# Fewer directly computed tiles ahead of the Strassen products in the FFNs of a two-layer trunk

## The chip, the cores and the metric

The kernel runs on one core of a Trainium2 chip, as one program. The metric is device time in microseconds (us). Numbers are float32 in and out.

## The reference

Two layers, each with three residual sub-layers: a SwiGLU feed-forward (FFN 1), a token mixer, and another SwiGLU (FFN 2). There are 512 tokens of width 1024; the inner width of an FFN is 2816.

```
def rms_norm(x, gain):
    inv = lax.rsqrt(jnp.mean(xf * xf, axis=-1, keepdims=True) + EPS)
    return (xf * inv).astype(x.dtype) * gain

def swiglu(h, w_in, w_out):
    gate, up = jnp.split(h @ w_in, 2, axis=-1)
    return (jax.nn.silu(gate) * up) @ w_out

for l in range(DEPTH):
    x = x + 0.5 * swiglu(rms_norm(x, ffn1_norm[l]), ffn1_w_in[l], ffn1_w_out[l])
    h = rms_norm(x, mix_norm[l]) @ w_mix_in[l]
    ...
    x = x + y @ w_mix_out[l]
    x = x + 0.5 * swiglu(rms_norm(x, ffn2_norm[l]), ffn2_w_in[l], ffn2_w_out[l])
```

## The kernel before

**Layout and precision.** The residual stream stands transposed in SBUF as `xT`: eight blocks of 128 channels by 512 tokens. A float32 product is made from two parts of each operand, a rounded high part (a cast on ScalarE, ACT) and the remainder (a subtraction on VectorE, DVE): high by high, high by low and low by high, three matmuls on TensorE (PE). So every weight tile that PE reads first passes ACT and then DVE; the pair lands in one of three buffers called `hl`.

**Two ways through the first matrix of an FFN.** The inner width is 22 tiles of 128, each with a gate and an up half. A pair of tiles can be computed directly, which the kernel calls *covered* (`cover`): 96 matmuls of 512 columns on the un-normalised `x` times the gain, in four steps of 24; the factor 1/rms per token is applied afterwards, when the bank is emptied ("clear", two multiplications by `inv` on DVE, then silu on ACT and "values", two products on DVE). Or a pair is computed as seven products after Strassen and Winograd (`halved`): P1 to P7, each 24 matmuls of 256 columns, 168 in all. These need the normalised `x` in four quarters `xn` (`normalise`), three sums of quarters ("+"), and from these seven operands `xc` (`operand`: a cast on ACT, a remainder on DVE). They also need sums of the weights' quarters q0 to q3: S1 to S4, S2 to S4 on DVE (`total`), and others by DMAs that add from memory (`add`, issued by GpSimd (POOL)).

**The entry of an FFN.** The inverse norm is not known when an FFN starts: the squares of the last channels are still to be summed. The covered tiles go first, because they need only `x`. Meanwhile the sum of squares is taken by a matmul with a matrix of 1/1024 (`squares`, `sum_norm`), then logarithm, exponential and a Newton step make `inv` (`take_norm`, `rsqrt`), and the quarters, sums and operands are made. What is due at which step is written out in the table `ENTRY`, under the number of covered tiles: a step number and a list of jobs. `deal(n)` issues the jobs of step n. While tiles are covered it is called with 2f + k // 2 (tile f, channel block k), four steps a pair; then with 2 * covered + n ahead of the first three weight preparations (`LEAD` = 3), and with the next numbers after each product. "load" starts the first unit of `halved`: four weight quarters by SP's queue, q2, q0, q3, q1 in order, and the addition of q3 to q2 (S1) by POOL's queue; "sum" is S2 on DVE. `prepare` casts one product's weights on ACT and takes its remainder on DVE, three products ahead of PE.

**Counts.** FFN 1 of layer 0 (the *opening*, in which `x` is also loaded and turned) covers six tiles, the three others four. In the opening, the sum of squares comes after the first covered pair; in FFN 1 of layer 1 `mean` = 2 and in FFN 2 `mean` = 3 say at which step it is dealt out.

**Order.** Tile schedules freely what is not tied; the kernel ties much of it: `follow(e, i)` appends instruction i to a hand-written chain of engine e ("a" ACT, "v" DVE, "p" PE, "s" SP's queue, "g" POOL's queue), so that the order of issue on each engine at an entry is that of the code. An instruction that waits therefore holds all that is behind it on its engine. The products of all later units run in an order that a planner (`plan`) made, with loads ahead.

**The opening's start.** Before data arrive PE multiplies zeros (`none`) by zeros (`idle`), two times and once more. The tile `none`, like `inv`, has the tag "inv" in a pool with one buffer per tag. In `norm_part` the square of a channel block is made by ACT into a tile `sq` of the rotating pool with several buffers, and added to `sqacc` by DVE.

Lines of the profile: L378 and L379 are cast and remainder of streamed weights, L392, L398 and L399 the three matmuls, L445 the first rows of the opening, L532 the addition of a square, L551 the sum by matmul, L300 activations (logarithm and exponential among them), L543 the last step of the Newton iteration, L643 and L644 "clear", L752 `normalise`, L774 and L775 ACT's and DVE's part of a negated operand, L816 the transfers that add weights from memory, L829 the sums of weights, L841 and L843 cast and remainder of a product's weights, L859 the addition of S2 to q1 by a transfer, L940 the copy of g2 in a silu.

Of the kernel before, what the change touches and what calls it, by code (L numbers as in the profile page):

```python
# [8 lines left out]
F32 = mybir.dt.float32  # L9
F32R = mybir.dt.float32r  # L10
# [3 lines left out]
AF = mybir.ActivationFunctionType  # L14
ALU = mybir.AluOpType
# [10 lines left out]
P = 128  # L26
T = 512
D = 1024
# [5 lines left out]
CHUNKS = ((0, 8), (8, 8), (16, 6))  # L34


ORDER_IN = ("P1", "P2", "P6", "P5", "P7", "P3", "P4")
ORDER_OUT = ("P2", "P1", "P5", "P6", "P7", "P3", "P4")
LEAD = 3

# [2 lines left out]


ENTRY = {
# [5 lines left out]
    },  # L51
# [5 lines left out]
    },  # L57
}

# [124 lines left out]
class Trunk:  # L184
# [8 lines left out]
    def __init__(self, ctx, tc):  # L193
        self.tc = tc
        self.nc = tc.nc
        nc = self.nc
        self.const = ctx.enter_context(tc.tile_pool(name="const", bufs=1))
        self.res = ctx.enter_context(tc.tile_pool(name="res", bufs=1))
        self.wp = ctx.enter_context(tc.tile_pool(name="wp", bufs=1))
        self.ps = ctx.enter_context(  # L200
            tc.tile_pool(name="ps", bufs=1, space=bass.MemoryType.PSUM)
        )
        self.dram = ctx.enter_context(
            tc.tile_pool(name="dram", bufs=1, space=bass.MemoryType.DRAM)
        )
        self.ident = self.const.tile([P, P], F32, tag="ident", name="ident")
        make_identity(nc, self.ident)
        self.ones_mean = self.const.tile([P, P], F32, tag="ones_mean", name="ones_mean")
        nc.vector.memset(self.ones_mean, 1.0 / D)
        self.epsc = self.const.tile([P, 1], F32, tag="epsc", name="epsc")  # L210
        nc.vector.memset(self.epsc, EPS)
        self.xT = self.res.tile([P, KD, T], F32, tag="xT", name="xT")

        self.none = self.res.tile([P, T], F32R, tag="inv", name="none")
        nc.vector.memset(self.none.bitcast(F32), 0.0)

        self.xh, self.xl = [None] * KD, [None] * KD
        self.uid = 0
        self.ntog = 0
        self.tab, self.tab_users = None, []  # L220
        self.chain = {}

    def build_consts(self, scratch):

# [182 lines left out]
    def stream_steps(  # L407
        self, jobs, parts_of, act, nk, mid=None, pre=None, deal=None, keep=False, lead=False,
        last=False, fine=False, deep=2, rowwise=False,
    ):  # L410

        k = 0
        while k < nk:
            kk = min(deep, nk - k)
            if callable(mid) and k == nk - 2:
                mid()
            st = None
            if pre is not None:  # L430

                if k == 0:
                    st = self.open_rows(parts_of(k, kk), kk)
                pre(k)
            if deal is not None:
                deal(k)
            skew = SKEW_MOVING if jobs[0][2] is not None and jobs[0][0].shape[-1] < T else 0
            if st is not None:

                def first(hi, lo):  # L440

                    ah, al = act(0)
                    for n, (w, x) in enumerate(((hi, ah), (lo, ah), (hi, al))):
                        for acc, cols, _ in jobs:
                            self.follow("p", self.nc.tensor.matmul(  # L445
                                acc, w[:, cols], x, start=n == 0, stop=False, skip_group_check=True
                            ))
                        if n == 0:
                            pre(k, None)

                self.between = first
            rows = self.granule(parts_of(k, kk), kk, pre is None, skew, deal is not None, st)
            if st is not None:
                self.first_rows = self.chain["v"]
            end = k + kk == nk
            halves = end and last
            order = (
                [(job, j) for job in jobs for j in range(kk)]
                if end and not rowwise or lead and k == 0
                else [(job, j) for j in range(kk) for job in jobs]  # L460
            )
            for n, ((acc, cols, toks, *more), j) in enumerate(order):
                if pre is not None and n == len(order) // 2:
                    pre(k, True)
                if fine and n == len(order) // 2:
                    yield
                if pre is not None and k + j == 0:
                    continue
                ah, al = act(k + j)
                hi, lo = rows[j]  # L470
                first, stop = k + j == 0 and not more, end and j == kk - 1
                if toks is None:
                    self.mm3(acc, hi[:, cols], lo[:, cols], ah, al, first, stop, False, keep)
                elif not (halves and acc is jobs[-1][0]):
                    self.mm3(
                        acc, ah[:, toks], al[:, toks], hi[:, cols], lo[:, cols], first, stop, False, keep
                    )
            if halves:
                acc, cols, toks = jobs[-1]
                for c in (slice(0, T // 2), slice(T // 2, T)):  # L480
                    for j in range(kk):
                        ah, al = act(k + j)
                        hi, lo = rows[j]
                        self.mm3(
                            acc[:, c], ah[:, toks], al[:, toks], hi[:, c], lo[:, c], False, j == kk - 1
                        )
            k += kk
            yield
# [20 lines left out]
    def norm_part(self, j, pool, xj=None, part=None):  # L509
# [16 lines left out]
        if j == 0:  # L526
            self.sqacc = self.res.tile([P, T], F32, tag="sqa", name=self.n("sqa"))
            nc.scalar.activation(self.sqacc, xj, AF.Square)
        else:
            sq = pool.tile([P, T], F32, tag=self.tt, name=self.n("sq"), bufs=self.tb)  # L530
            nc.scalar.activation(sq, xj, AF.Square)
            nc.vector.tensor_add(self.sqacc, self.sqacc, sq)  # L532

# [93 lines left out]
    def cover(self, fp, w_in, w_out, covered, mean, begin):  # L627
# [35 lines left out]
        def deal(n):  # L663
            if n == mean and begin is None:
                squares()
            for what in filter(None, ENTRY[covered].get(n, "").split(", ")):
                name, *at = what.split()
                at = [int(v) if v.isdigit() else v for v in at]
                if name == "norm":
# [23 lines left out]
        for f in range(0, covered, 2):  # L693
            banks = self.next4()

            def parts(k, kk, f=f):
# [6 lines left out]
                [(bk, slice(c, c + P), None) for bk, c in zip(banks, (0, 256, 128, 384))],  # L703
                parts, self.xact, KD, None,
                (lambda *a: self.open_x(x, gain, fp, *a)) if opening else None,
                None if opening else (lambda k, f=f: deal(2 * f + k // 2)), begin is None or f > 2,

                lead=f == 2 and begin is not None,
            )
# [71 lines left out]
    def halved(self, fp, w_in, w_out, covered, deal):  # L781
# [49 lines left out]
        def prepare(kind, w, p):  # L831
# [7 lines left out]
            hl = self.wp.tile([P, 2 * 1024 + 64], F32R, tag="hl", name=self.n("hl"), bufs=3)  # L839
            hi, lo = (hl[:, a + SKEW_HELD : a + SKEW_HELD + 1024] for a in (0, 1024))  # L840
            A(nc.scalar.copy(hi, src))  # L841
            parts[u, p] = [a.rearrange("p (k c) -> p k c", k=4) for a in (hi, lo)]
            return lambda: V(nc.vector.tensor_sub(lo, src, hi))  # L843

        def moving(c, p):

# [40 lines left out]
                do[name](*args)  # L887

        u = seq[0][:2]
        for q in (2, 0, 3, 1):  # L890
            raw[u, q] = t = fp.tile(
                [P, 4, 2 * P], F32, tag=("mh", "ml")[q % 2], name=self.n("w"), bufs=2
            )
# [821 lines left out]
    def open_x(self, x, gain, fp, k, loaded=False):  # L1715
# [5 lines left out]
            return  # L1721
        if not loaded:
            if k == 0:
                self.idle(2)
                self.begin_norm(gain, fp)
                self.table(LNEXP)
                self.follow("a", self.tab_ins)
                self.xb = {0: self.load_x(x, 0, fp)}
                self.load_open(0)
                self.idle(1)  # L1730
                self.xb[1] = self.load_x(x, 1, fp, True)
                self.load_open(1)
            self.norm_part(k, fp, self.xb[k], 0)
# [8 lines left out]

    def idle(self, n):

        for _ in range(n):
            b = self.bank("po")
            self.follow("p", self.nc.tensor.matmul(b, self.none[:, :P], self.none, start=True, stop=True))

    def open_rest(self, j, fp):
# [25 lines left out]
def trunk_kernel(  # L1775
# [4 lines left out]
    k = Trunk(ctx, tc)  # L1780
    for l in range(DEPTH):
        k.ffn(
            ffn1_w_in[l], ffn1_w_out[l], mix_norm[l], 4 if l else 6, 2,
            begin=(x, ffn1_norm[0]) if l == 0 else None,
        )
        k.mix(
# [1 line left out]
            fox_k_gain[l], fox_f_bias[l], ffn2_norm[l], hgrn_lb_logits,  # L1788
        )
        k.ffn(  # L1790
            ffn2_w_in[l], ffn2_w_out[l], ffn1_norm[l + 1] if l + 1 < DEPTH else None, 4, 3,
            out=out if l + 1 == DEPTH else None,
        )

# [28 lines left out]
```

## Time and profile before

| what | us |
|---|---|
| median of 3 runs | 1830.18 |
| lowest and highest | 1828.83, 1830.91 |
| the profiled execution, its time | 1832.37 |
| the profiled execution, its span | 1830.6 |

The profile is one execution, taken by the hardware profiler. The span runs from its first to its last instruction. PE is TensorE's matmuls, PEld its weight loads (they run beside matmuls), DVE VectorE, ACT ScalarE, POOL GpSimd, SP SyncE; "x" and a number are instructions. A row of the timeline has the start in us, the duration in us (of all of them, where x4 at the end of the row stands for four in a run), the engine, the line, the operation, the tiles written and read, their sizes, and in brackets how long the engine stood idle before it and what ended that. A row of windows has the stretch, its length, and for each engine asked for (PE alone, or PE, PEld, DVE, ACT and POOL) the busy time and in brackets the number of instructions, then the granted clock of TensorE (1.00 is full), the DMA engines' busy share and the GB/s moved. The mean granted clock was 1.00. The transfers of the whole execution:

```profile
q1 hardware_dynamic: 193904, 192.15, 35.7%
q0 software_dynamic: 55840, 68.19, 23.4%
HBM read 226.15 MB, written 2.17 MB: 125 GB/s over the span
```

q1 are the transfers that SP issues, q0 those that POOL issues: packets, MB, and their share of 16 DMA engines' span.

### The profile page before, as it was taken

How to read it: one execution, taken by the hardware profiler on the slowest of the kernel's cores; microseconds unless marked ns; L12 is line 12 of the kernel's file. 1: busy time of each engine (PE TensorE's matmuls, PEld its weight loads, DVE VectorE, ACT ScalarE, POOL GpSimd, SP SyncE). 2: the span in 40 equal slices, each digit the busy share in tenths (PEclk: the TensorE clock that was granted, in tenths of full speed). 3: DMA queues.
4: the chain of work that ended last, by engine and by line, in shares of the span. 5: the costliest groups of instructions: out<-in, count | busy, mean ns of one | idle time of the engine just before them, and what ended most of it. 6: DMA issues, size and time to landing. Idle time of an engine off the chain costs nothing.

```text
span 1830.6 us, 31999 instructions
## 1 busy us (share of the span) xinstructions
PE 1821.0 (99%) x12934; PEld 1674.7 (91%) x12934; DVE 1445.3 (79%) x1965; ACT 1001.7 (55%) x1414; POOL 185.1 (10%) x190
## 2 busy tenths in 40 slices
PE   9999999999999999999999999999999999999999
PEld 7899999888888899999889999998888888999997
DVE  8889786679677888879678887976777778888883
ACT  5455554465666465555445555555656655555552
POOL 0011120100000101112001111201000001020210
PEclk9999999999999999999999999999999999999999
DMA  7668783242543767868276787823425438677762
GB/s 214 177 134 189 177 180 94 68 124 68 127 110 96 216 136 168 193 165 174 81 202 140 174 183 190 163 69 84 114 74 127 119 98 217 161 152 196 154 135 92
DMA packets 249908, 262.38 MB, mean 143 GB/s; under 512 B 19816, under 2 KB 228464, under 8 KB 249760
## 3 DMA queue, kind: packets, MB, share of 16 engines
q1 hardware_dynamic: 193904, 192.15, 35.7%
q0 software_dynamic: 55840, 68.19, 23.4%
q8 instruction: 101, 1.65, 0.4%
q14 instruction: 47, 0.39, 0.1%
q10 hardware_dynamic: 16, 0.00, 0.0%
HBM read 226.15 MB, written 2.17 MB: 125 GB/s over the span
## 4 chain that ended last, share of the span: by engine, by line
PE 96%; ACT 1%; DVE 1%; DMA 1%; issue 0%; SPq 0%; DVEq 0%; ACTq 0%
PE mm L392 14%; PE mm L399 14%; PE mm L398 14%; PE sc L392 6%; PE sc L399 6%; PE sc L398 6%; PE pt L392 6%; PE pt L399 6%; PE pt L398 6%; PE po L392 4%; PE po L399 4%; PE po L398 4%; PE sc L1600 1%; PE po L1655 1%; PE sc L1414 1%; PE pt L1637 1%
## 5 line engine op out<-in xcount | busy, mean ns | idle before, releaser
L841 ACT CAST hl<-w 128x1024 fp32r<-128x1024 f32 x322 | 337.7, 1050 | 347.6 <-PE mm L399 81.9
L843 DVE TENSOR_TENSOR hl<-w,hl 128x1024 fp32r<-128x1024 f32 x322 | 392.5, 1220 | 87.2 <-ACT hl L841 87.0
L379 DVE TENSOR_TENSOR hl<-st,hl 128x1024 fp32r<-128x1024 f32 (+3 forms) x152 | 160.0, 1053 | 120.4 <-ACT hl L378 119.7
L378 ACT CAST hl<-st 128x1024 fp32r<-128x1024 f32 (+3 forms) x152 | 138.6, 912 | 176.3 <-PE po L399 81.5
L392 PE MATMUL mm<-xc,hl 128*128 128x256 f32 (+1 forms) x730 | 201.4, 276 | 0.3 <-ACT g L940 0.3
L399 PE MATMUL mm<-xc,hl 128*128 128x256 f32 x728 | 201.4, 277 | 0.0
L398 PE MATMUL mm<-xc,hl 128*128 128x256 f32 x728 | 201.2, 276 | 0.0
L392 PE MATMUL sc<-xc,hl 128*128 128x256 f32 (+1 forms) x530 | 146.4, 277 | 0.6 <-ACT g L940 0.6
L399 PE MATMUL sc<-xc,hl 128*128 128x256 f32 x528 | 146.1, 277 | 0.0
L398 PE MATMUL sc<-xc,hl 128*128 128x256 f32 x528 | 146.0, 277 | 0.0
L392 PEld LDWEIGHTS mm<-xc,hl 128*128 128x128 f32 x730 | 137.0, 188 | 0.8 <-ACT g L940 0.5
L398 PEld LDWEIGHTS mm<-xc,hl 128*128 128x128 f32 x728 | 136.8, 188 | 0.0
L399 PEld LDWEIGHTS mm<-xc,hl 128*128 128x128 f32 x728 | 136.6, 188 | 0.1
L392 PE MATMUL pt<-xc,hl 128*128 128x256 f32 (+1 forms) x482 | 132.7, 276 | 0.0
L398 PE MATMUL pt<-xc,hl 128*128 128x256 f32 x480 | 132.7, 276 | 0.0
L399 PE MATMUL pt<-xc,hl 128*128 128x256 f32 x480 | 132.6, 276 | 0.0
L392 PE MATMUL mm<-x,hl 128*128 128x512 f32 x272 | 108.8, 400 | 0.0
L399 PE MATMUL mm<-x,hl 128*128 128x512 f32 x272 | 106.1, 390 | 0.0
L398 PE MATMUL mm<-x,hl 128*128 128x512 f32 x272 | 105.9, 389 | 0.0
L392 PEld LDWEIGHTS sc<-xc,hl 128*128 128x128 f32 x530 | 99.5, 188 | 1.5 <-ACT g L940 1.0
L399 PEld LDWEIGHTS sc<-xc,hl 128*128 128x128 f32 x528 | 99.2, 188 | 0.1
L398 PEld LDWEIGHTS sc<-xc,hl 128*128 128x128 f32 x528 | 99.1, 188 | 0.0
(487 smaller groups left out, 5470.6 us busy)
## 6 DMA issues: line engine op xcount, KB each, us to landing
w<-in_ffn_w_in_dram SPq DMA_DIRECT2D x140, 512.0 KB
w<-in_ffn_w_out_dram SPq DMA_DIRECT2D x64, 512.0 KB
w<-in_ffn_w_out_dram POOLq DMA_DIRECT2D x56, 512.0 KB, 9.0
st<-in_w_mix_in_dram SPq DMA_DIRECT2D x80, 256.0 KB
w<-in_ffn_w_in_dram POOLq DMA_DIRECT2D x39, 512.0 KB, 8.1
st<-in_ffn_w_in_dram SPq DMA_DIRECT2D x70, 256.0 KB
w<-S POOLq DMA_DIRECT2D x35, 512.0 KB, 4.7
st<-in_ffn_w_out_dram SPq DMA_DIRECT2D x24, 512.0 KB
```

The source lines that it names most:

```text
L378: a = nc.scalar.copy(hi, src[:, c : c + w])
L379: b = nc.vector.tensor_sub(lo, src[:, c : c + w], hi)
L392: i = nc.tensor.matmul(acc[:, c], ah, bh[:, c], start=first and c.start == 0, stop=False, skip_group_check=True,)
L398: nc.tensor.matmul(acc, ah, bl, start=False, stop=False, skip_group_check=True)
L399: i = nc.tensor.matmul(acc, al, bh, start=False, stop=last, skip_group_check=True)
L841: A(nc.scalar.copy(hi, src))
L843: return lambda: V(nc.vector.tensor_sub(lo, src, hi))
L1414: nc.tensor.matmul(s2[:, :, t], e[:, i * P : (i + 1) * P], e2[:, :, t], start=True, stop=True)
L1600: mm = lambda *a, **k: E(nc.tensor.matmul(*a, skip_group_check=True, **k))
L1637: E(nc.tensor.transpose(tb[:, k * P : (k + 1) * P], to[u][:, j * P : (j + 1) * P], self.ident))
L1655: E(nc.tensor.matmul(self.ob[:, o], half[2][:, j, h].rearrange("p a d -> p (a d)"), part[:, at[0] : at[-1] + 1, :].rearrange("p b t -> p ( ...
```

## The change

- The opening covers four tiles, not six; the other three FFNs cover two, not four. What is no longer covered goes through the seven products, one pair more in each FFN.
- `ENTRY` has a table for two covered tiles and one named "opening"; the old two are gone. `deal` is also called in the middle of a step (n + 0.5), so that a job can stand at a half step ("load" at 3.5; the sum of squares of layer 1's FFN 1 at `mean` = 1.5). In FFN 2 the sum of squares stands at step 2.
- P5 comes before P6 in the order of products in the first matrix.
- Where two tiles are covered, the remainders of the first two weight preparations (P1 and P2 of the first unit) aren't made by DVE: ACT writes the negated rounded weights to the low part, and a DMA issued by POOL adds the weights to it.
- The first unit's quarters are loaded in the order q2, q0, q1, q3.
- The squares in `norm_part` go to one buffer, that of the tag "inv".
- In the opening the zeros are written first, there are four and three matmuls on them, not two and one, and each group writes one bank, not a new one each time. The chains begin with the zeros' and the ones' memset on DVE.

```diff
-ORDER_IN = ("P1", "P2", "P6", "P5", "P7", "P3", "P4")
+ORDER_IN = ("P1", "P2", "P5", "P6", "P7", "P3", "P4")
...
 ENTRY = {
-    4: {
-        5: "norm, x 0 0", 6: "x 1 0, P1", 7: "load, x 0 1, + 0 0 0 1, P2", 8: "sum, x 1 1, P5",
-        9: "clear 0, + 0 0 1 1", 10: "silu 0, + 0 1 1 1, P6, P7", 11: "values 0, clear 1",
-        12: "silu 1, P3", 13: "+ 0 0 1 0, values 1", 14: "P4", 17: "clear 2", 18: "silu 2",
+    2: {
+        3.5: "load", 4: "norm, x 0 0", 5: "P1, x 1 0", 6: "P2, x 0 1, + 0 0 0 1, P5, sum",
+        7: "x 1 1, + 0 0 1 1, + 0 1 1 1, P6", 8: "P7", 9: "P3, + 0 0 1 0", 10: "P4", 12: "clear 0",
+        13: "silu 0", 14: "values 0, clear 1", 15: "silu 1", 16: "values 1",
+    },
+    "opening": {
+        6: "norm", 7: "load, x 0 0, x 1 0, P1", 8: "x 0 1, + 0 0 0 1, P2", 9: "clear 0, sum",
+        10: "P5, x 1 1", 11: "+ 0 0 1 1, P6, clear 1", 12: "silu 0, + 0 1 1 1, P7", 13: "values 0, P3",
+        14: "silu 1, + 0 0 1 0, P4", 15: "values 1", 17: "clear 2", 18: "silu 2",
         19: "values 2", 20: "clear 3", 21: "silu 3", 22: "values 3",
-    },
-    6: {
-        7: "norm, x 0 0", 8: "x 1 0, clear 0, clear 1", 9: "silu 0, silu 1, x 0 1, P1, + 0 0 0 1",
-        10: "load, P2, values 0, values 1, x 1 1", 11: "P5, clear 2, + 0 0 1 1",
-        12: "silu 2, P6, clear 3, sum", 13: "values 2, silu 3, + 0 1 1 1, P3", 14: "P7, values 3, + 0 0 1 0",
-        15: "P4", 16: "clear 4", 17: "silu 4", 18: "values 4, clear 5", 19: "silu 5", 20: "values 5",
     },
 }
...
+        self.none = self.res.tile([P, T], F32R, tag="inv", name="none")
+        self.follow("v", nc.vector.memset(self.none.bitcast(F32), 0.0))
         self.ident = self.const.tile([P, P], F32, tag="ident", name="ident")
...
-        nc.vector.memset(self.ones_mean, 1.0 / D)
+        self.follow("v", nc.vector.memset(self.ones_mean, 1.0 / D))
...
+                if deal is not None and n == len(order) // 2:
+                    deal(k, 0.5)
...
-            sq = pool.tile([P, T], F32, tag=self.tt, name=self.n("sq"), bufs=self.tb)
+            sq = self.res.tile([P, T], F32, tag="inv", name=self.n("sq"))
             nc.scalar.activation(sq, xj, AF.Square)
             nc.vector.tensor_add(self.sqacc, self.sqacc, sq)
...
             A(nc.scalar.copy(hi, src))
+            byload = covered == 2 and u == seq[0][:2] and p in ("P1", "P2")
+            if byload:
+                A(nc.scalar.activation(lo, src, AF.Copy, scale=-1.0))
+                G(nc.gpsimd.dma_start(lo.bitcast(F32), src, accum_op=ALU.add))
...
-            return lambda: V(nc.vector.tensor_sub(lo, src, hi))
+            return lambda: byload or V(nc.vector.tensor_sub(lo, src, hi))
...
-        for q in (2, 0, 3, 1):
+        for q in (2, 0, 1, 3):
...
-                self.idle(2)
+                self.idle(4)
...
-                self.idle(1)
+                self.idle(3)
...
+        b = self.bank("po")
         for _ in range(n):
-            b = self.bank("po")
...
-            ffn1_w_in[l], ffn1_w_out[l], mix_norm[l], 4 if l else 6, 2,
+            ffn1_w_in[l], ffn1_w_out[l], mix_norm[l], 2 if l else 4, 1.5,
...
-            ffn2_w_in[l], ffn2_w_out[l], ffn1_norm[l + 1] if l + 1 < DEPTH else None, 4, 3,
+            ffn2_w_in[l], ffn2_w_out[l], ffn1_norm[l + 1] if l + 1 < DEPTH else None, 2, 2,
```

More of the change, by code (lines that the diff above doesn't have):

```diff
@@ L196, in __init__ @@
         nc = self.nc
+        self.uid = 0
+        self.ntog = 0
+        self.tab, self.tab_users = None, []
+        self.chain = {}
         self.const = ctx.enter_context(tc.tile_pool(name="const", bufs=1))
@@ L212, in __init__ @@
         self.xT = self.res.tile([P, KD, T], F32, tag="xT", name="xT")
-        self.none = self.res.tile([P, T], F32R, tag="inv", name="none")
-        nc.vector.memset(self.none.bitcast(F32), 0.0)
         self.xh, self.xl = [None] * KD, [None] * KD
[L218 to L221, printed above, removed]
     def build_consts(self, scratch):
@@ L665, in deal @@
                 squares()
-            for what in filter(None, ENTRY[covered].get(n, "").split(", ")):
+            for what in filter(None, ENTRY[covered if begin is None else "opening"].get(n, "").split(", ")):
                 name, *at = what.split()
@@ L705, in cover @@
                 (lambda *a: self.open_x(x, gain, fp, *a)) if opening else None,
-                None if opening else (lambda k, f=f: deal(2 * f + k // 2)), begin is None or f > 2,
+                None if opening else (lambda k, half=0, f=f: deal(2 * f + k // 2 + half)), begin is None or f > 2,
                 lead=f == 2 and begin is not None,
```

## The prediction

> **What bounds the kernel now.** I read the page first (engines, slices, chain), then windows of single stages, then the timeline of one entry into an FFN.
>
> ```profile
> span 1830.6 us, 31999 instructions
> PE 1821.0 (99%) x12934; PEld 1674.7 (91%) x12934; DVE 1445.3 (79%) x1965; ACT 1001.7 (55%) x1414; POOL 185.1 (10%) x190
> PEclk9999999999999999999999999999999999999999
> PE 96%; ACT 1%; DVE 1%; DMA 1%; issue 0%; SPq 0%; DVEq 0%; ACTq 0%
> ```
>
> TensorE (PE) works in 99% of the span and is 96% of the chain of waits: nothing but its matmuls sets the end. So there are two ways to change the time: fewer PE microseconds, or new pauses of PE. The change does the first on purpose; the question is what it does to the second, and for that a 79% share of VectorE (DVE) says little. It has to be read at the entry of an FFN.
>
> ```profile
> 57.14:78.90 21.76, 21.76 (x98) 1.00 0.79 221
> 78.90:98.07 19.17, 19.17 (x170) 1.00 0.48 108
> 593.35:616.00 22.65, 22.65 (x100) 1.00 0.68 194
> 614.78:637.75 22.97, 22.97 (x103) 19.00 (x102) 22.90 (x32) 10.06 (x11) 3.45 (x3) 1.00 0.84 234
> ```
>
> In these windows the first time after the stretch is PE's busy time; in the last row PEld's and then DVE's (22.90) follow. The first row is a pair of covered tiles (96 matmuls of 512 columns), the second a pair in seven products (168 of 256 columns), the third a covered pair with the norm's sum in it. The fourth is the stretch between the finished inverse norm and the first product of layer 0's FFN 2: DVE has 0.07 us free in 23 us. What it does there (normalising, operands, remainders) is what the products need, and two covered pairs give it the time.
>
> **What is saved.** A pair that goes from covered to products saves 21.76 - 19.17 = 2.59 us of PE. Four pairs move (one in each FFN): 10.4 us. The built order agrees: 672 more matmuls of 256 columns (4 x 168) and 384 fewer of 512, beside 4 more on zeros.
>
> **What the shorter cover exposes, FFN 2 of either layer.** Rows of layer 0's entry, PE, ACT and DVE:
>
> ```profile
> 593.35 0.39 PE L392 MATMUL sc<-x,hl 128*128 128x512 f32 x1
> 603.35 0.69 DVE L532 TENSOR_TENSOR sqa<-sqa,sq 128x512 f32<-128x512 f32 x1
> 609.67 1.02 PE L551 MATMUL po<-sqa,ones_mean 128*128 128x512 f32 x2
> 610.79 0.69 ACT L300 ACTIVATE nr<-po,epsc 128x512 f32<-128x512 f32 x1 [5.30 <-PE po L551]
> 613.76 1.28 ACT L293 ACT_TABLE_LOAD   x1
> 614.09 0.69 DVE L543 TENSOR_TENSOR inv<-nr,nt 128x512 f32<-128x512 f32 x1
> 614.81 1.67 DVE L752 SCALAR_TENSOR_TENSOR xn<-xT,gain,inv 128x256 f32<-128x256 f32 x4
> 616.40 1.22 DVE L379 TENSOR_TENSOR hl<-st,hl 128x1024 fp32r<-128x1024 f32 x1
> 616.52 1.06 ACT L774 ACTIVATE xc<-xn 128x1024 fp32r<-128x1024 f32 x1 [1.47 <-DVE xn L752]
> 617.54 1.67 DVE L752 SCALAR_TENSOR_TENSOR xn<-xT,ngain,inv 128x256 f32<-128x256 f32 x4
> 619.12 1.22 DVE L775 SCALAR_TENSOR_TENSOR xc<-xn,xc 128x1024 fp32r<-128x1024 f32 x1
> ```
>
> From starts: four normalising steps take 1.59 (614.81 to 616.40), an operation on 128x1024 takes 1.14 (616.40 to 617.54) and is done after 1.22; ACT's part of an operand is done after 1.06; the logarithm starts 1.12 after the sum (609.67 to 610.79) and the inverse is ready 3.99 after that (614.78).
>
> Count from the start of the cover (593.35 = 0). The sum is now called at step 2 of 4, not 3 of 8: at 10.9, where the last square has just been added (604.04, or 10.7; the squares now share one buffer, so each waits for the addition before it, but only the last one or two by some 0.1). Logarithm 12.0, inverse 16.0. The cover ends at 22.65 (third row of the windows) and the products start there, 2.74 each.
>
> DVE's order is fixed by hand; the built one gives, from the inverse on: normalise (0,0); remainder of operand P1; normalise (1,0); remainder P2; normalise (0,1); an addition; remainder P5; S2; weight remainders P5, P6; normalise (1,1); two additions; remainder P6. That is 4 x 1.59 + 9 x 1.14 + 1.22 = 17.8, and three times DVE stands 1.1 for ACT's half of an operand that has just been normalised: 21.4, with the small gaps 21.7. So P6's operand is whole at 16.0 + 21.7 = 37.7, and P6, the fourth product, wants it at 22.65 + 3 x 2.74 + 0.1 = 31.0: **6.7 late** (P5 takes the first 3 of them). Then P7: its weights are q0 plus a transfer that can only be issued after S2 (30.2).
>
> ```profile
> w<-in_ffn_w_in_dram POOLq DMA_DIRECT2D x39, 512.0 KB, 8.1
> w<-S POOLq DMA_DIRECT2D x35, 512.0 KB, 4.7
> DMA to landing us min/median/max: 4.5/4.7/7.2
> ```
>
> Landed 38.4, cast 39.5, remainder 40.7, and the remainder of operand P7 behind it on DVE 42.3; P7 could start at 40.4: 1.8 more. P4 loses 0.6 in the same way. Sum **9.1 us of new pauses against 2.59 saved: +6.5 for each FFN 2**.
>
> The two remainders made by transfers cost ACT two casts with a sign (1.06 each, by the L774 row) and POOL two issues; the table load that used to lie behind a cast now ends at 15.3, so P1's second cast ends at 17.3. For their landing no row shows a copy of w into hl; the nearest is w<-S, 4.7 in the median (third row: 4.5 to 7.2), and the slowest POOL row, 15.0 for additions from memory, is the far end. At 4.7 P1 and P2 land at 22.1 and 25.4, on time; at 7.2 they are 2 late, and the chain to P6 swallows that. I take 0.
>
> **FFN 1 of layer 1.**
>
> ```profile
> 919.31 0.39 PE L392 MATMUL mm<-x,hl 128*128 128x512 f32 x1
> 925.45 0.68 DVE L532 TENSOR_TENSOR sqa<-sqa,sq 128x512 f32<-128x512 f32 x1
> DMA to landing us min/median/max: 5.7/8.3/15.0
> ```
>
> Here the squares are added at 926.13, 6.8 after the cover's start, and the sum goes out at step 1.5, at 8.2. All of the chain is 2.7 earlier, the transfer of P7 included; where it waited for buffers it gains less: **6.6 of pauses, +4.0 net**.
>
> **The opening (layer 0, FFN 1).**
>
> ```profile
> 34.21 1.04 ACT L378 CAST hl<-st 128x1024 fp32r<-128x1024 f32 x1 [2.18 <-DMA st<-in_ffn_w_in_dram]
> 36.53 0.68 ACT L300 ACTIVATE nr<-po,epsc 128x512 f32<-128x512 f32 x1
> 45.42 0.68 DVE L644 TENSOR_TENSOR ui<-sc,inv 128x512 f32<-128x512 f32 x1
> L445 PE MATMUL sc<-x,hl 128*128 128x512 f32 x6 | 3.5, 680 | 1.0 <-ACT hl L378 1.0
> L398 PE MATMUL sc<-x,hl 128*128 128x512 f32 x14 | 5.5, 390 | 0.0
> ```
>
> The logarithm is moved one cast forward, to 35.3, behind the cast that waits for a load (34.21). The inverse is ready at 39.2. P1 starts at 57.14, after the second covered pair. In the built order DVE has, before P5 may start, the two remainders of the cover, the operands up to P6, weight remainders, S2 and, last, "clear 1", which empties the bank that P5 writes: 13 x 1.14 + 4 x 1.59 + 3 x 0.6 = 23 and 4 of waits for ACT, to 66.3. P5 wants it at 62.6: 3.7 late. P7's addition and operand and P4's come behind: 2.3 more. **6.0 of pauses, +3.4 net.**
>
> The zeros: matmuls of 512 columns took 680 ns before 12.3 us, 390 after. Twelve of them stand there, 0.2 apart in pace, so 2.4 us are to be had at most, and 0 if the clock opens no earlier. But the logarithm hangs on a load (the 2.18 of the L378 row), so a faster PE meets the same 66.3 unless loads come earlier too. I take half, -1.2, and keep 0 and -2.9 (with the transposes) as ends. Loads, the additions' order and the buffer of the squares elsewhere I cost at nothing: PE hides them, and where DVE has no slack they are in the chains above. In the pairs behind an entry DVE catches up (some 17 of 19 us); 0, up to 0.5 an entry.
>
> **Sum.** 2 x 9.1 + 6.6 + 6.0 - 10.4 - 1.2 = **+19.2 us**. The profiled execution has a span of 1830.6 and a time of 1832.37; the median of the runs is 1830.18, 0.4 below that span. I put the change on the median: **1849.4**.
>
> **Rivals.**
>
> *The lead suffices (faster).* If the operands were ready when PE asks, only the saving stays: 1830.18 - 10.4 - 1.2 = 1818.6. For it: the sum is as early as the squares allow, two DVE operations are gone from the entry, and PE has no long wait today. Against: it needs 30 us less lateness over four entries, and the order of DVE with durations seen in dozens of rows leaves little room; it decides at 2.9 of pauses an entry. 14%.
>
> *Half and half.* P6's lateness stays, the rest is hidden, and the zeros pay: 2 x 6.7 + 4 + 3.7 - 10.4 - 2.9 = +7.8, 1838. It is the low end of the forecast.
>
> *The clock falls in the pauses (slower still).* Each entry gets pauses of 2 to 4 us on PE; today's longest past the start is below 1:
>
> ```profile
> PE sc L445 <- ACT hl L378: 1.0, 1, 1.0
> PE sc L392 <- ACT g L940: 0.6, 2, 0.3
> ```
>
> If the clock drops as at the start, some 6 us (6.35 to 12.3) at 390/680 of the pace lose about 2.6 an entry, less what DVE's lateness covers: +8, 1857. 14%. The Trainium skill has a rule for it: "TensorE: Matmul & The Clock Gate", section "HAM oscillation — how this bites in real kernels", says that idle gaps of PE above some 3.4 us put the clock back to half. No trace here has such a gap yet; by that rule the opening's 3.7 us would trip it and FFN 2's two gaps, with one matmul between, might.
>
> *The transfers decide.* Beside the next pair's loads the two remainders land after 10 to 15 us; P2 then has its weights at 33.7 and the chain to P6 is no longer the later one: +3 for each of three entries, 1858. 6%.
>
> **How the numbers follow.** Forecast with its low end 63%, clock 14%, transfers 6%, faster 14%, and 3% for pauses that just eat the saving. The range holds the forecast from its low end (22.6 of pauses, zeros at their best: 1839, and a little for shorter waits) to the two slower rivals: 1836 to 1861. Within 0.2% (3.7 us) nothing can be told from no change. Faster 0.14, same 0.03, slower 0.83.
>
> **What would show it.** In the profile after: pauses of PE of 2 to 4 us behind the covered pair, ended by DVE's xc (P6) at FFN 2's entries and by gi in the opening; 7 products taking some 28 us in FFN 2, 26 in layer 1's FFN 1, 25 in the opening, not 19.2; a P7 cast ended by a DMA of w. A clock row below 9, or a PE wait on hl ended by a DMA, would speak for the slower rivals. I am wrong if the seven products of an entry take less than 22 us, or if DVE is idle while PE waits.

## The result and the profile after

The changed kernel takes 1923.43 us (median of 4 runs, 1918.33 to 1925.94) against 1829.93 (4 runs, 1828.83 to 1830.91): a ratio of 1.0508, 95% interval 1.0485 to 1.053. The forecast was slower by 19; it became 93. The page of the changed kernel's profile:

```profile
span 1921.0 us, 32645 instructions
PE 1842.0 (96%) x13226; PEld 1705.8 (89%) x13226; DVE 1466.7 (76%) x1967; ACT 1026.0 (53%) x1444; POOL 199.1 (10%) x204
PEclk9899999999999999999999999999999998999999
```

PE is down from 99% to 96% of a longer span, so some 79 us of it are pauses (1921.0 - 1842.0; 9.6 before), and its clock row, all nines before, has two eights, in the slices of the opening and of layer 1's FFN 2 entry. PE's waits, by what ended them:

```profile
PE mm L391 <- ACT g L947: 29.5, 12, 4.9
PE po L391 <- ACT g L947: 10.5, 6, 2.2
PE sc L391 <- ACT g L947: 6.7, 3, 3.4
PE mm L398 <- DMA hl<-w: 6.6, 3, 2.7
PE pt L391 <- ACT g L947: 5.1, 2, 3.4
PE mm L391 <- ACT xc L781: 5.0, 3, 2.2
PE pt L391 <- DVE gi L645: 3.9, 1, 3.9
PE mm L397 <- DVE xc L781: 2.6, 3, 0.9
```

(Total, times, longest.) The four rows without g are what the prediction spoke of: operands (xc), a bank to be emptied (gi), a transfer (hl<-w). The four rows with g, 51.8 us in 23 waits, are one thing that it did not speak of: ACT's copy g2 (L947, L940 before), which empties the bank of P6. Four of these waits, 9.9 us, lie in the first units, the other 19 behind them. One of them, in the middle of layer 0's FFN 2 (timeline, PE, ACT and DVE):

```profile
698.36 0.28 PE L398 MATMUL mm<-xc,hl 128*128 128x256 f32 x1
698.71 1.04 ACT L843 CAST hl<-w 128x1024 fp32r<-128x1024 f32 x1 [1.17 <-issue]
699.66 0.59 ACT L947 ACTIVATE g<-mm 128x512 f32<-128x512 f32 x1
699.79 1.23 DVE L850 TENSOR_TENSOR hl<-w,hl 128x1024 fp32r<-128x1024 f32 x1 [1.49 <-ACT hl L843]
...
700.31 0.38 PE L391 MATMUL mm<-xc,hl 128*128 128x256 f32 x1 [1.67 <-ACT g L947]
```

The first row is P6's last matmul, the last row P7's first. P7 adds into the bank that P6 wrote, so it must wait until ACT has copied P6's sum out. The copy is behind the cast of the weights for the product three ahead, and that cast can only begin when P6 frees its weight buffer. 1.04 and 0.59 and what lies between them make 1.95 from matmul to matmul. DVE stands idle meanwhile (1.49), waiting for the same cast. Before, P5 stood between P6 and P7, wrote another bank and gave ACT 2.7 us:

```profile
666.30 1.05 ACT L841 CAST hl<-w 128x1024 fp32r<-128x1024 f32 x1
667.26 0.59 ACT L940 ACTIVATE g<-pt 128x512 f32<-128x512 f32 x1
669.02 1.05 ACT L841 CAST hl<-w 128x1024 fp32r<-128x1024 f32 x1 [1.17 <-issue]
669.98 0.59 ACT L943 ACTIVATE u<-sc 128x512 f32<-128x512 f32 x1
```

The first two rows are the same two steps, cast and then P6's copy, with nothing waiting for them: they run beside P5. The next two are the cast and the copy behind P5, and they run beside P7. In the changed kernel P7 comes right behind P6 in 19 of the 35 later units; in the others the planner has put products of the second matrix between them, and no such pause is there.

The first products of each FFN (windows: the stretch, its length, PE's busy time and count, the granted clock, the DMA engines' share and GB/s):

```profile
55.56:86.78 31.22, 23.94 (x171) 0.84 0.39 81
634.58:664.38 29.80, 22.38 (x171) 0.94 0.59 119
984.57:1012.19 27.62, 22.09 (x170) 0.94 0.64 140
1582.38:1614.78 32.40, 24.68 (x170) 0.84 0.54 110
```

The forecast was 25, 28, 26 and 28 us. One reason is in the clock's column: 0.84 to 0.94 there.

**Where the 90.4 us of span are.** From the starts of successive matmuls of all products: at full pace they are 0.113 us apart; what a distance has above that counts as a pause where it is over 0.25 us, as half pace between 0.13 and 0.25 (most of these are at 0.21). The first unit of each FFN is "entry", the rest "behind".

| us | before | after |
|---|---|---|
| pauses, entries | 1.9 | 31.3 |
| half pace, entries | 1.0 | 12.5 |
| pauses behind | 0 | 47.2 |
| half pace behind | 1.3 | 14.1 |
| a pace of 0.118, all | 2.4 | 4.9 |
| pairs moved to products | | -10.4 |
| opening's first two covered pairs | | -1.6 |

The -10.4 is four times the difference of the two windows of before. The rows after less those before make 91.4, 1.0 more than the 90.4; the table doesn't hold the rest of the program. Two covered pairs of the opening end at 55.56, 1.58 earlier than the 57.14 of before.

### The profile page after: what moved, and what is told of

It is laid out like the page before. It is cut to its first block, busy times and chain, and to the rows that moved or that the text cites. A ratio compares the mean times of both kernels' runs of the same rounds, so it can differ in the third digit from the quotient of the medians.

```text
span 1921.0 us, 32645 instructions
## 1 busy us (share of the span) xinstructions
PE 1842.0 (96%) x13226; PEld 1705.8 (89%) x13226; DVE 1466.7 (76%) x1967; ACT 1026.0 (53%) x1444; POOL 199.1 (10%) x204
## 5 line engine op out<-in xcount | busy, mean ns | idle before, releaser
L391 PE MATMUL mm<-xc,hl 128*128 128x256 f32 (+1 forms) x1251 | 354.0, 283 | 34.5 <-ACT g L947 29.5
L398 PE MATMUL mm<-xc,hl 128*128 128x256 f32 x1248 | 352.3, 282 | 6.6 <-DMA hl<-w 6.6
L397 PE MATMUL mm<-xc,hl 128*128 128x256 f32 x1248 | 352.3, 282 | 2.6 <-DVE xc L781 2.6
L391 PEld LDWEIGHTS mm<-xc,hl 128*128 128x128 f32 x1251 | 241.6, 193 | 37.8 <-ACT g L947 32.0
L398 PEld LDWEIGHTS mm<-xc,hl 128*128 128x128 f32 x1248 | 241.4, 193 | 7.3 <-DMA hl<-w 7.1
L397 PEld LDWEIGHTS mm<-xc,hl 128*128 128x128 f32 x1248 | 241.1, 193 | 3.2 <-DVE xc L781 3.2
L391 PE MATMUL po<-xc,hl 128*128 128x256 f32 (+1 forms) x435 | 121.8, 281 | 10.5 <-ACT g L947 10.5
L397 PE MATMUL po<-xc,hl 128*128 128x256 f32 x432 | 121.2, 280 | 0.0
L398 PE MATMUL po<-xc,hl 128*128 128x256 f32 x432 | 120.9, 280 | 0.0
L818 POOL DMA_DIRECT2D w<-in_ffn_w_out_dram x56 | 73.8, 1396 | 248.6 <-DVE hl L850 137.6
L818 POOL DMA_DIRECT2D w<-in_ffn_w_in_dram x43 | 70.1, 1631 | 260.3 <-DMA w<-in_ffn_w_in_dram 81.0
L391 PEld LDWEIGHTS po<-xc,hl 128*128 128x128 f32 x435 | 82.9, 191 | 11.8 <-ACT g L947 11.8
L391 PE MATMUL sc<-m,hl 128*128 128x256 f32 x336 | 93.2, 277 | 0.0
L397 PE MATMUL sc<-m,hl 128*128 128x256 f32 x336 | 93.1, 277 | 0.0
L398 PE MATMUL sc<-m,hl 128*128 128x256 f32 x336 | 93.0, 277 | 0.0
L391 PE MATMUL pt<-m,hl 128*128 128x256 f32 x336 | 93.0, 277 | 0.0
L397 PE MATMUL pt<-m,hl 128*128 128x256 f32 x336 | 93.0, 277 | 0.0
## 6 DMA issues: line engine op xcount, KB each, us to landing
w<-in_ffn_w_in_dram POOLq DMA_DIRECT2D x43, 512.0 KB, 10.4
```

The lines of the kernel that those rows point to most:

```text
L391: i = nc.tensor.matmul(acc[:, c], ah, bh[:, c], start=first and c.start == 0, stop=False, skip_group_check=True,)
L397: nc.tensor.matmul(acc, ah, bl, start=False, stop=False, skip_group_check=True)
L398: i = nc.tensor.matmul(acc, al, bh, start=False, stop=last, skip_group_check=True)
L818: G(nc.gpsimd.dma_start(raw[u, q], src(u, q2), accum_op=ALU.add))
```

## The experiments

All times beside runs of the kernel before on the same chip (medians 1830.35, 1830.8 and 1830.37 in the three sets).

### The order of P5 and P6

**P6 first again, everywhere (`order_back`).**

```diff
-ORDER_IN = ("P1", "P2", "P5", "P6", "P7", "P3", "P4")
+ORDER_IN = ("P1", "P2", "P6", "P5", "P7", "P3", "P4")
```

> The changed kernel with P6 ahead of P5 again in all units; all else as changed. Theory (the bank): P7 adds into the bank that ACT copies after P6; with P5 between them the copy was hidden, without it PE waits 1.95 to 5.2 us in 23 later units (43.8 us, and 14.4 more of slow P7s), some 56 us in all behind the entries, and in the four first units too. So the time falls by 56 behind the entries and by 4 x 1.9 or more in them: 1853 to 1862. Rival (a late engine): the entries leave ACT, DVE or the transfers late, and the waits on the copy only show it; then the order gives back little: 1900 or more, and the same waits stand before P5 or P7.

1875.36 us (1866.79 to 1876.42), ratio 1.0234 [1.0207, 1.026]: 48 less than the changed kernel. Pauses behind the entries 2.9 us, not 47.2; half pace there 1.6, not 14.1. The rival falls. (The 23 units of the expectation are 19 later units and the four first ones.) The time is above the expected range for two reasons: the entries still have 45.7 us in all, so the old order gives nothing back there, and in layer 1's FFN 2 of the profiled run PE kept a pace of 0.118 us (below), 9 us.

**P5 first in the first unit only (`order_first_only`).**

```diff
+FIRST_IN = ("P1", "P2", "P5", "P6", "P7", "P3", "P4")
+ORDER_IN = ("P1", "P2", "P6", "P5", "P7", "P3", "P4")
...
-        ("I", f, p) for f in range(max(covered, c[0]), c[0] + c[1], 2) for p in ORDER_IN
+        ("I", f, p) for f in range(max(covered, c[0]), c[0] + c[1], 2) for p in (FIRST_IN if f == covered else ORDER_IN)
```

> The changed kernel with P5 ahead of P6 in the first unit of an FFN alone, P6 first in all later units. Theory (the bank): only the 56 us behind the entries go, the four entries keep their 44 us: 1863 to 1871; against the run with the old order everywhere this tells what the order is worth at the entry: 2 to 14 us for the old one. Rival (P5 first is right at the entry, since P6's operand is late): this one is faster than the old order everywhere, by up to 2.7 an entry. Rival (a late engine): 1900 or more.

1866.79 us (1862.76 to 1872.58), ratio 1.0203 [1.0182, 1.0225], in the expected range: 56.6 us less. Entries 44.1 us by the trace, against 45.7 with the old order: at the entry the order is worth about nothing, since P5's work fills a wait for P6's operand and P7 then waits for P6's copy. The difference of this run's time to the run above can't be told from the slow pace.

**The copy ahead of the cast, new order kept (`copy_ahead`).**

```diff
+            if kind == "I" and p == "P6":
+                work[u, "g2"] = g2 = tmp("g2")
+                A(nc.scalar.activation(g2, acc, AF.Copy, scale=-1.0))
             rest = prepare(*seq[n + LEAD]) if n + LEAD < len(seq) else None
...
             elif p == "P6":
-                work[u, "g2"] = g2 = tmp("g2")
-                A(nc.scalar.activation(g2, acc, AF.Copy, scale=-1.0))
+                pass
```

> The changed kernel with ACT's copy of P6's bank issued ahead of the cast of the weights for the product three ahead; new order kept. Theory (the bank): the cast waits for the buffer that P6 itself sets free, takes 1.05 us and stands ahead of the copy; with the copy first, the pause before P7 falls from 1.95 to 0.9 in every unit, those of 3.7 to 5.2 as well, and no P7 is slow any more: 23 x 0.9 = 21 us are left behind the entries, 1884 to 1892. Rival (a late engine, or PE held by something else than the copy): under 10 us of gain, 1913 or more.

1876.27 us (1871.45 to 1879.91), ratio 1.0251 [1.0232, 1.027]: 47 less, more than expected. Its waits at three of the four banks:

```profile
PE mm L391 <- ACT g L927: 10.0, 12, 2.2
PE po L391 <- ACT g L927: 4.9, 5, 1.2
PE sc L391 <- ACT g L927: 3.7, 3, 2.4
```

Behind the entries 17.7 us of pauses are left of 47.2 and 2.5 of half pace of 14.1: the distance from P6 to P7 is 0.96, not 1.95, in most units, and 1.5 at most, not 5.2. So the cast ahead of the copy made half of the usual wait and most of what the long ones had more; the rest is the copy itself.

**The new order alone, in the kernel before (`before_p5_first`).**

```diff
-ORDER_IN = ("P1", "P2", "P6", "P5", "P7", "P3", "P4")
+ORDER_IN = ("P1", "P2", "P5", "P6", "P7", "P3", "P4")
```

> The kernel before with nothing changed but P5 ahead of P6. Theory (the bank): the same waits as in the changed kernel, in one unit fewer per FFN: some 11 us behind each entry and 1.9 or more in each first unit: 1875 to 1890, slower than before by 45 to 60. Rival (a late engine after the short cover): with the long cover nothing is late, so within 10 us of before.

1888.71 us (1884.85 to 1891.39), ratio 1.0319 [1.0304, 1.0334]: 58 slower than before by this line alone, with the long cover and no operand late. Its four kinds of waits on the copy:

```profile
PE mm L392 <- ACT g L940: 14.3, 7, 3.6
PE pt L392 <- ACT g L940: 11.2, 4, 4.3
PE sc L392 <- ACT g L940: 9.3, 6, 1.8
PE po L392 <- ACT g L940: 5.3, 2, 3.6
```

40.1 us in 19 waits, and 14.8 of half pace behind the entries. Three waits for "clear" (gi, L643), 3.3 us, come at the entries, where P5 now wants its bank sooner. These three sums make the 58.

### The small edits

**The zeros alone, in the kernel before (`zeros_only`).**

```diff
+        self.none = self.res.tile([P, T], F32R, tag="inv", name="none")
+        self.follow("v", nc.vector.memset(self.none.bitcast(F32), 0.0))
         self.ident = self.const.tile([P, P], F32, tag="ident", name="ident")
...
-                self.idle(2)
+                self.idle(4)
...
-                self.idle(1)
+                self.idle(3)
...
+        b = self.bank("po")
         for _ in range(n):
-            b = self.bank("po")
```

> The kernel before with the new start alone: zeros written first, four and three matmuls on them, in one bank. In the changed kernel the second covered pair of the opening ended at 55.56, before at 57.14. If that is the zeros' doing it shows here too: 1.2 to 2.0 us less than the kernel before, 1828.2 to 1829.0, and the loss of the changed kernel has no part from it. Rival: the earlier end came from the other loads or the shorter opening; then 0.3 or less.

1828.9 us (11 runs), ratio 0.999 [0.9981, 0.9999]: 1.9 less, as expected. The matmuls of the first rows, groups by line of this kernel's opening:

```profile
L445 PE MATMUL sc<-x,hl 128*128 128x512 f32 x6 | 2.6, 514 | 0.1
L445 PE MATMUL pt<-x,hl 128*128 128x512 f32 x6 | 2.0, 417 | 0.0
```

The six of the first row took 680 ns each before, now 514: PE reaches its pace earlier. The clock's column doesn't show this: in the kernel before it reads 1.00 from the start, through these slow matmuls too, so the pace there is read from durations.

**The earlier sum alone, in the kernel before (`sum_early`).**

```diff
-            ffn1_w_in[l], ffn1_w_out[l], mix_norm[l], 4 if l else 6, 2,
+            ffn1_w_in[l], ffn1_w_out[l], mix_norm[l], 4 if l else 6, 1.5,
...
-            ffn2_w_in[l], ffn2_w_out[l], ffn1_norm[l + 1] if l + 1 < DEPTH else None, 4, 3,
+            ffn2_w_in[l], ffn2_w_out[l], ffn1_norm[l + 1] if l + 1 < DEPTH else None, 4, 2,
```

(With the half steps in `deal`.)

> The kernel before with the sum of squares dealt out earlier alone (step 1.5 in FFN 1 of layer 1, 2 in FFN 2). In the kernel before each entry behind a cover of four loses 0.8 to 0.9 us in its first unit, most of it before P7, while VectorE has no slack. If the end of the inverse sets VectorE's chain, an inverse some 3 us earlier makes that vanish: 0 to 2.5 us less, 1827.7 to 1830.2. Rival: the sum now waits for the last squares and stops PE: up to 1.5 us an entry more, 1830 to 1835.

1830.77 us, ratio 1.0 [0.9991, 1.0008]. Both were wrong: nothing stops PE, but the 0.9 us at each entry stay, before the same P7. When the inverse is ready doesn't set what is left there.

**All but counts, tables, order and transfers (`all_but_counts_and_order`).** The two edits above together with

```diff
-            sq = pool.tile([P, T], F32, tag=self.tt, name=self.n("sq"), bufs=self.tb)
+            sq = self.res.tile([P, T], F32, tag="inv", name=self.n("sq"))
...
-        for q in (2, 0, 3, 1):
+        for q in (2, 0, 1, 3):
```

> The kernel before with the small edits of the change: new start, early sum, one buffer for the squares, loads in the order q2, q0, q1, q3. Not with it: the covered counts and their tables, the order of P5 and P6, the remainders by transfers. If the prediction was right to cost these at nothing but the zeros: 1826 to 1829.5. Rival: the squares in one buffer hold ACT and VectorE before the entries (three waits of 0.5 to 1 us each): 1831 to 1834.

1828.92 us, ratio 0.9988 [0.998, 0.9997]: what the zeros give, and nothing for the rest.

### The entries

**Remainders of P1 and P2 by DVE (`remainders_by_dve`)**, on `order_first_only`:

```diff
-            byload = covered == 2 and u == seq[0][:2] and p in ("P1", "P2")
+            byload = False and u == seq[0][:2] and p in ("P1", "P2")
```

> The changed kernel with P5 first in the first unit only (1866.8 so far) and with the remainders of P1 and P2 by VectorE as everywhere else, no transfers for them. Theory (VectorE's chain sets the entry): P1 no longer waits 3 us for a transfer in the three entries, but two operations of 1.14 us come ahead of P6's operand: between 2.3 less and 2.3 more an entry, 1860 to 1873, with the wait now before P6. Rival (the transfers set it): 3 us less an entry and the half clock after it gone too, 1858 or less.

1862.85 us (1860.89 to 1868.14), ratio 1.0177 [1.0162, 1.0193]. The waits for the transfers (6.4 us, P1 or P2 of three entries) are gone, and the entries have 44.8 us where they had 44.1: P5 and P6 wait instead, for VectorE. Who makes these two remainders only moves the wait. By the medians the run is 3.9 less, but the ranges of the two kernels overlap, and the entries don't show it.

**Two additions less (`two_additions_less`)**, on `order_first_only`:

```diff
-        7: "x 1 1, + 0 0 1 1, + 0 1 1 1, P6", 8: "P7", 9: "P3, + 0 0 1 0", 10: "P4", 12: "clear 0",
+        7: "x 1 1, P6", 8: "P7", 9: "P3, + 0 0 1 0", 10: "P4", 12: "clear 0",
...
-        10: "P5, x 1 1", 11: "+ 0 0 1 1, P6, clear 1", 12: "silu 0, + 0 1 1 1, P7", 13: "values 0, P3",
+        10: "P5, x 1 1", 11: "P6, clear 1", 12: "silu 0, P7", 13: "values 0, P3",
```

> The same kernel without the two additions that make the quarters of x for P6 and P7's operand (+ 0 0 1 1 and + 0 1 1 1 are left out, so P6, P7 and P4 of every pair take other numbers). VectorE has 2 x 1.14 us less ahead of P6's operand at each of the three short entries, and as much in the opening ahead of P6 and P7. Theory (VectorE's chain sets the entry): 2.0 to 2.5 us less an entry and a part of the half clock: 8 to 14 us less than 1866.8, 1853 to 1859. Rival (transfers or ACT's casts set it): under 3 us less.

1861.34 us (1858.44 to 1864.02), ratio 1.0167 [1.0153, 1.0181]: 5.4 less, between the two. The trace divides it: PE's wait ahead of P6 is gone at two of the short entries and down from 3.7 to 1.3 at the third (layer 1's FFN 2), so VectorE's chain did set that one, but these entries have 34.1 us in all where they had 33.2; only the opening has less, 7.6 for 10.9. The rest of the 5.4 may be runs of the other kernel at the slow pace (below); no trace shows it. ACT at layer 0's FFN 2 in this run:

```profile
632.23 1.05 ACT L844 CAST hl<-w 128x1024 fp32r<-128x1024 f32 x1 [3.62 <-DMA w<-in_ffn_w_in_dram]
...
635.26 1.04 ACT L844 CAST hl<-w 128x1024 fp32r<-128x1024 f32 x1 [0.51 <-DMA w<-S]
636.22 0.59 ACT L951 ACTIVATE u<-mm 128x512 f32<-128x512 f32 x1
636.71 1.03 ACT L782 CAST xc<-xn 128x1024 fp32r<-128x1024 f32 x1
637.64 1.04 ACT L844 CAST hl<-w 128x1024 fp32r<-128x1024 f32 x1
638.59 0.60 ACT L948 ACTIVATE g<-mm 128x512 f32<-128x512 f32 x1
```

The cast of P7's weights waits for the addition from memory (issued only after S2), everything else of ACT stands behind it, P6's copy last; P7 waits 5.1 us for that. At the short entries this second limit lies right behind VectorE's, and takes all that the first gave back.

**The pauses filled (`pauses_filled`)**, on `order_first_only`, with a tile of zeros `zw` (32 columns):

```diff
+FILL = {2: 8, 3: 20, 4: 16}
...
             acc = work[u, k]
+            if n in FILL:
+                to, x = work[u, "b" if p == "P7" else "a"], self.xc["P1"][0][:, 0, :]
+                for i in range(FILL[n]):
+                    self.follow("p", nc.tensor.matmul(
+                        to[:32, :H], self.zw, x, start=False, stop=False, skip_group_check=True
+                    ))
```

> The changed kernel with P5 first in the first unit only (1866.8 so far), and matmuls on zeros put in front of the first unit's P5 (8), P6 (20) and P7 (16), added to a bank that nobody reads then: 5.0 us of work an entry at 0.113 us each, less than the pauses there. In that kernel some 118 matmuls of the entries ran at the half pace (0.21 us), 11.5 us in all. Theory (the clock falls in the pauses): with the pauses filled most of it goes; what VectorE's chain had hidden of it comes back as waits, so 3 to 9 us less: 1858 to 1864, and under 40 matmuls at the half pace. Rival (the half pace has another cause, or the wait for VectorE just grows by it): within 3 us, or slower by the zeros, 1864 to 1872.

1859.31 us (1859.11 to 1859.6), ratio 1.0156 [1.014, 1.0171]: 7.5 less by the medians, 3.7 by the fastest runs; in the traces the first units of the four entries are 4.5 us shorter (120.9 to 116.4), although each has 44 matmuls more. Matmuls at half pace at the entries: 49, not 118, a little over the expected 40. Layer 0's FFN 2, first products, without and with the zeros (windows):

```profile
622.03:653.79 31.76, 23.73 (x170) 0.89 0.57 115
```

```profile
620.19:649.86 29.67, 25.43 (x215) 1.00 0.60 120
```

The granted clock goes from 0.89 to 1.00 and the stretch is 2.1 us shorter. So the pauses cost twice: as pauses, and by the clock behind them.

### A version ahead of both

**Zeros and the copy ahead, in the kernel before (`before_zeros_copy`).** The edits of `zeros_only` and of `copy_ahead`.

> The kernel before with the new start (zeros) and with ACT's copy of P6's bank issued ahead of the cast of the next weights; counts and order as before. In the kernel before each entry behind a cover of four loses 0.9 us in its first unit, of which 0.47 is P7's wait for that copy, behind two casts. Theory (the bank): these three waits go too: 1.9 + 1.4 less than before, 1827.0 to 1828.2. Rival: the wait before P7 is for the operand or the weights and stays: 1828.5 to 1829.5; the later cast costs nothing, since PE does not wait for it.

1829.87 us (11 runs), ratio 0.9996 [0.9987, 1.0005]. P7's waits are gone, and at each of the three entries a new pause of 1.06 us stands before P4, 0.9 of it a wait that VectorE's addition to u2 ended: the wait moved from P7 to P4. Nothing gained; the zeros alone stay the best, 1.9 us below the kernel before.

## Why the prediction was wrong

**Right.** The saving, 10.4, and PE's time of a pair; the zeros (-1.2 forecast, -1.6 in the trace, -1.9 alone). The chain at the entry: from the cover's start at 611.83 in layer 0's FFN 2 the forecast had the inverse at 16.0 and P6's operand whole at 37.7. The trace has (VectorE's timeline)

```profile
627.21 0.69 DVE L545 TENSOR_TENSOR inv<-nr,nt 128x512 f32<-128x512 f32 x1
...
648.63 1.23 DVE L781 TENSOR_TENSOR xc<-xn,xc 128x1024 fp32r<-128x1024 f32 x1
```

that is 16.1 and 38.0. P7's operand came at 41.5 (forecast 42.3), and in the opening P5 started at 65.2 (forecast 66.3). (Its sum of DVE's work adds up to 21.1, not the 21.4 that it gives; the trace has 22.0.) That the earlier sum, the squares' buffer and the order of loads cost nothing is right as well.

**Right in part by luck.** The entries' pauses, 9.1 + 6.6 + 9.1 + 6.0 = 30.8, are 31.3 in the trace, but they are made of other waits. 6.6 us are waits of P1 and P2 for the transferred remainders, taken at nothing; the chain to P6 swallowed these, as the prediction said of a late landing. 9.9 us are P7's waits for P6's copy (3.4 in the opening, then 1.7, 1.7 and 3.1), which the prediction didn't have: it had P7's weights and operand there. That layer 0's FFN 2 shows 1.84 before P7 where 1.8 was forecast is chance: the operand was whole 2.8 us earlier, and the copy ended the wait.

**Wrong, the large one.** The sum had no term for the new order of P5 and P6; the step that went through the parts of the change took it only as the order in which operands are asked for at the entry. It is a change in every unit where nothing else stands between P6 and P7, 19 of the 35 later ones: it takes away the product that stood between P6's copy and P7's write to the same bank. That is 47.2 us of pauses behind the entries and 14.1 of half pace: `before_p5_first` has 58 us by it alone, `order_first_only` gets 57 back. The sentence "In the pairs behind an entry DVE catches up", with its "0, up to 0.5 an entry", looked at VectorE; the wait was on ACT and a bank. Before's page had hints: the copy g2 was among PE's few waits, and a look at which product writes which bank would have priced it: a cast of 1.05 and a copy of 0.59 in a row with the gaps around them, 1.8 us, in 23 units (19 later, four first), an estimate of 41 us.

**Wrong, the smaller one.** The clock was a rival with 14% and +8. It fell at all four entries (12.5 us) and behind six of the later waits. Of the eight distances of 1.9 us and more at the entries, five were followed by half pace, so it belonged in the forecast: without the order, the sum would have been 1849.4 + 11.5 (12.5 less before's 1.0) = 1860.9. `order_first_only` and `remainders_by_dve` measured 1866.8 and 1862.9. The rule quoted from the Trainium skill ("TensorE: Matmul & The Clock Gate", "HAM oscillation — how this bites in real kernels") was right in kind: all 24 pauses with a distance of starts above 3.2 us were followed by half pace, but so were 23 of 34 between 2.1 and 3.2 (the counts are in the last section).

**The rivals.** "The lead suffices" is out by every run: with the old order or the new, the kernels with the short cover are slower than before by 29 us or more. "Half and half" (1838) is out with it. "The transfers decide" is half seen: P1 or P2 waited for its remainder in three entries (6.6 us), but without those transfers the wait only moved; the ones behind S2 are a second limit for P7.

What stays open: whether the short cover could pay at all with P7's weights prepared earlier and P6's copy out of ACT's way (not tried together), and the slow pace below.

## What to carry to other kernels

When an order of accumulating steps is changed, write down beside each step which bank it writes and who must have read that bank: a copy-out is hidden only by a step that writes elsewhere, and it also waits for all that stands ahead of it in its own engine's queue. Count such an edit by the number of units that run in that order, not by the place for which it was made. And where a change makes pauses of more than 2 us on TensorE, price them with the half pace behind them; work on zeros in the pauses took 69 of 118 slow matmuls away here.

## What the runs showed of the hardware

**The clock can fall after pauses of little more than 2 us.** After one of the pauses (windows of the changed kernel, granted clock in the fourth column):

```profile
675.30:677.70 2.40, 0.25 (x3) 1.00 0.69 216
677.70:679.00 1.30, 1.29 (x6) 0.55 0.60 163
679.00:680.00 1.00, 1.00 (x7) 0.50 0.92 320
...
681.00:682.15 1.15, 1.15 (x10) 0.89 0.79 273
```

A pause of some 2.2 us, then some 3.5 us at half. Over the eight traces that have such pauses, by the distance of starts, and counted as followed when at least 8 of the next 25 matmuls ran at some 0.21 us:

| distance, us | pauses | followed by half pace |
|---|---|---|
| 1.9 to 2.1 | 30 | 1 |
| 2.1 to 2.5 | 15 | 11 |
| 2.5 to 3.2 | 19 | 12 |
| above 3.2 | 24 | 24 |

So the length alone doesn't decide between 2.1 and 3.2. In the changed kernel the pause at the start of layer 0's FFN 2 (634.75, a distance of 3.04) left the granted clock at 1.00; so did the other six of the 19 that weren't followed. All seven are P1's wait for its transferred remainder at the start of an FFN 2, but five other waits of P1, 2.7 to 3.2 long, were followed. What decides stays open.

**A second, slower pace.** In some FFNs of some runs all products ran at 0.118 us a matmul, not 0.113, with the granted clock at 1.00. Two stretches of `order_first_only`, FFN 2 of layer 0 and FFN 1 of layer 1:

```profile
700.00:750.00 50.00, 50.00 (x426) 1.00 0.71 165
1050.00:1100.00 50.00, 50.00 (x444) 1.00 0.77 161
```

18 matmuls fewer in 50 us, 4%, over 245 us: 9 us of that run. There it begins at a short pause (at 665.5, 0.77 us) and ends with the FFN. A pause isn't needed: the kernel before has two shorter stretches at this pace, from 283.5 and from 1762.1, over 20 us each; one distance of some 0.22 us stands at their start, no pause. The 9 us are about the whole spread among the runs of that kernel (1862.76 to 1872.58), but no trace here shows one of its faster runs. What sets the pace wasn't tried.
